# A hybrid mixing layer with a SwiGLU network: stores put off by a tile, a product order changed, and the passage into gate/up rearranged

## The chip, the cores and the metric

The kernel runs on one core of one Trainium2 chip. The metric is the device time of one execution in microseconds, the median over the runs. The engines are named as in the profile: PE (TensorE, matmuls), PEld (its weight loads), DVE (VectorE), ACT (ScalarE), POOL (GpSimd) and SP (SyncE, which here issues nearly all DMAs). Each engine takes its instructions in order, so an instruction that waits holds up everything behind it in its engine's queue. "The granted clock" is the share of full speed at which PE was allowed to run; its two levels here are 1.2 and 2.4 GHz (0.5 and 1.0).

## The reference, cut to what matters

There are 2048 tokens of width 1024, one sequence, one layer, float32.

```python
mod = silu(c) @ ada_w + ada_b            # six vectors: shift, scale, gate, twice
h = x * (1 + scale_m) + shift_m
z = h @ w_in                             # 512 columns each of cg, xin, bg, q, k, v, g
y_conv = bg * conv3(cg * xin)            # short causal convolution over tokens
q, k = rotary(q), rotary(k) * 128**-0.5  # 4 heads of 128
r = head_norm(retention(q, k, v))        # chunks of 128 tokens, decaying state
mix = concat(y_conv, silu(g) * r) @ w_out
x = layernorm(alpha * x + gate_m * mix) * ln1_g + ln1_b
h = x * (1 + scale_f) + shift_f
ff = (silu(h @ w_gate) * (h @ w_up)) @ w_down      # inner width 2816
out = layernorm(alpha * x + gate_f * ff) * ln2_g + ln2_b
```

## The kernel before, in words

**Arithmetic.** Each large product is made of three float16 matmuls that add up in float32: both operands are split into a rounded part (hi) and the rest (lo), and `mm3` (L135 to L137) issues hi·hi, hi·lo and lo·hi. A split is one ACT instruction (L130, hi) and one DVE instruction (L131, lo). The convolution's projection and gate/up multiply 2 x 2 blocks with seven products and not eight, so sums and differences of blocks (called planes for the activations) are made beforehand and the products are combined afterwards. A product is 12 matmuls of 512 columns, a gemm of the retention 24.

**Memory.** SBUF is cut into 24 pages of 128 x 2048 float32. `free` puts a page at the end of a list and `page` takes one from its front; `page(at=-1)` takes the last one, that which was freed most recently. Whoever writes a page waits for what still reads it, so the place in the list at which a page is freed decides whose transfer waits for whose.

**Order.** A planner puts the instructions of each engine in order by a simulated time, with the order of the program as the priority. `tc.issue_after(ins)` places what its block issues, on the engine of `ins`, behind that instruction.

**Stages.** After a start of some 125 us, the *retention* goes by tiles t of 128 tokens, t = 4 to 15, to some 460 us. A tile has four gemms (`gemm_ret(t, u)`: q, k, v, g), each evicted from PSUM into the tile's page: u = 0 by DVE (L705), u = 1 and 2 by ACT (L709), u = 3 by ACT with Silu (L711). Around them stand the rotary of t (L734 to L736 on DVE, then POOL), the transposes of t - 1 (L753, DMAs issued on SP), the scores of t - 1 (masked by DVE, L767), the state (L782), and y of t - 2 (matmuls L793, statistics L800 and L802, L804 to L807 on POOL, L810 on DVE), its transposed store through `ret_mix` (L832). Two tiles form a pair p; on every even tile the next pair's x, loaded at L231 on SP, is modulated (`ret_h`, L296, on ACT for p > 3) and split (`ret_hsplit`). The convolution needs seven planes of every pair. They are made in the tiles too: `h_more` stores the planes of the first split, makes sums on POOL (L344 to L347), splits them, and stores the other planes; `h_store` (L356) issues these DMAs on ACT. The pairs 4 to 7 leave this as a closure in `chores`; the pairs 0 to 3, whose x is loaded again, do it in the tiles 7, 10, 11 and 13 (`h_again`). The conditioning weights come through `ada_load` (on SP, `page(at=-1)`) and are summed by DVE (`ada_sum`, L199).

The *convolution* (some 460 to 710 us) has 12 pairs of a column block and a half of the tokens; each makes its seven products in the order 0, 5, 4, 1, 6, 3, 2 (`conv_pair`), with evictions on DVE (L973, L978, L982, L984) and ACT (L971, L975). Product 6 adds into the PSUM bank of product 5, product 1 into that of product 0, product 2 into that of product 4.

The *out-projection* (to some 875 us) goes over pairs of token tiles j = 0, 1, 4, 5, 6, 7, 2, 3. `op_half` adds one half (0: convolution, 1: retention) to y (L1307 on DVE), `norm1` normalises (statistics L1267 on DVE, scaling L1278 on ACT), `y_store` keeps y in DRAM (L1327), `h2_pair` scales it for the network (L1341 on DVE, L1342 on POOL) and makes the planes (L1347 to L1355), `h2_turn` transposes them (L1374, SP).

In the *passage* the weights of the first column blocks q of gate/up are scaled and split (`gu_split1`: L1412, L1413; `gu_split2`: differences L1421 to L1423, then L1426 on ACT and L1427 on DVE), and the first three blocks run: `gu(0, 1)`, `gu(1, 1)` and, once the last pair is there, `gu(0, 0)`. `gu` makes its seven products in the order A11, S2, S1, A12, A22, S3, S4; S3 adds into the bank of S2, which DVE first reads into u2 (L1465); S4 adds into that of S1 and A12 into that of A11, which ACT reads first (L1467, L1463). Gate/up runs to some 1590 us and the down-projection with the second norm to the end.

Of the kernel before, what the change touches and what calls it, by code (L numbers as in the profile page):

```python
# [11 lines left out]
F16 = mybir.dt.float16  # L12
# [28 lines left out]
def kernel(ctx: ExitStack, tc: tile.TileContext, xT, x, c, adaN, adaT, ada_b, w_ret, w_conv,  # L41
                             conv_w, w_out, ln1, ln1c, w_gu, w_dn, ln2, rope, consts, out):
    nc = tc.nc
# [340 lines left out]
    chores = []  # L384

    def h_more(p, pg, h):
        h_store(p, h, (0, 1, None, 3))
        h_sums(pg)
        g, _ = h_split(pg, hs[:, 0:1])
        h_store(p, g, (5, 2, 6, 4))  # L390
        free(pg, g)

    def h_again(p):

        pg = xt_pg.pop(p)
        for k in range(KT):
            modulate(pg.rearrange("p (k n) -> p k n", k=KT), k, True)
        h, _ = h_split(pg, hs[:, 0:1])
        h_more(p, pg, h)
        free(h)  # L400
# [288 lines left out]
    T1 = {}  # L689

    def gemm_ret(t, u):
# [258 lines left out]
    def conv_pair(u, b, done=lambda m: None):  # L950
# [125 lines left out]
    for t in range(4, NT):  # L1076
# [15 lines left out]
        gemm_ret(t, 1)  # L1092
        if t % 2 == 1 and p < 7:
            xt_load(p + 1)
# [23 lines left out]
        if end:  # L1118
            free(ropep, *ret_pages[4:6])
            hp_load(0, 4)  # L1120
            hp_load(0, 1)
            hp_load(0, 6)
        if t % 2 == 0 and p < 8:
            ret_h(p)
            ret_hsplit(p)
# [3 lines left out]
        if end:  # L1129
            free(*ret_pages[6:8])  # L1130
            hp_load(0, 3)
# [39 lines left out]
    ahead = [0, 5, 4, 1, 6, 3, 2]  # L1171
# [102 lines left out]
    def norm1(y):  # L1274
# [3 lines left out]
        nc.scalar.activation(y, y, AF.Identity, scale=rs, bias=nm)  # L1278
# [50 lines left out]
    def h2_pair(j, tp=None):  # L1329
# [4 lines left out]
        fp = yp[j] if tp else page()  # L1334
# [74 lines left out]
    def gu_split1(q):  # L1409
# [5 lines left out]
        gu_w[q] = {"A11": av[:, :, 0], "A12": av[:, :, 1], "S1": av[:, :, 2], "A22": av[:, :, 3], "pages": [wa]}  # L1415

    def gu_split2(q, eng):
        pg = gu_stage.pop(q)
# [10 lines left out]
        w = gu_w[q]  # L1429
# [8 lines left out]
    u32, ucount, gu_last, gu_pe = [], [0], [None], [None]  # L1438
# [3 lines left out]
    def gu(q, bl, between=None):  # L1442
# [28 lines left out]
        nc.scalar.activation(u[:, 0], pa, AF.Silu, scale=iv_g)  # L1471
        pd = new()
        prod(pd, "A22", T4, True, True)
        prod(pb, "S3", T3, False, True)
# [4 lines left out]
        prod(pc, "S4", B22, False, True)  # L1479
        nc.vector.tensor_add(u2, pc, u2)  # L1480
# [175 lines left out]
    order = (0, 1, 4, 5, 6, 7, 2, 3)  # L1656
    for i, j in enumerate(order):
# [10 lines left out]
        if i == 7:  # L1668
# [8 lines left out]
            gu_split2(0, nc.gpsimd)  # L1677
        for t in (2 * j, 2 * j + 1):
            if i < 7:
                op_half(t, 0)  # L1680
            op_half(t, 1)
            norm1(ytile(t))
# [8 lines left out]
        else:  # L1691
            y_store(j)
        if i == 5:
            gu_load(1)
    free(*wo_pages[2:])
    for i in range(2):
        gu_pages[i].append(page(F16, at=-1))
    gu_split1(1)
    gu_split2(1, nc.vector)
    free(*gu_pages[2])  # L1700
    gu_pages[2].clear()
    gu(0, 1)
# [11 lines left out]
    gu(1, 1)  # L1714
# [3 lines left out]
    gu_scale(2)  # L1718
# [4 lines left out]
    gu_scale(3)  # L1723
# [176 lines left out]
```

## Time and profile before

| | |
|---|---|
| median of 3 runs | 2106.2 us (2104.92 to 2108.79) |
| profiled execution | 2106.87 us |
| its span, first to last instruction | 2104.7 us |
| mean granted clock | 0.987 |
| matmuls | 9631 |
| data moved by DMA | 361.06 MB, 172 GB/s |

The span is what the trace covers; the execution's own time has some 2 us more around it. A busy time sums what an engine worked; an idle time before an instruction is shown in brackets with what ended it.

### The profile page before, as it was taken

To read this page: it belongs to the slowest core of one execution; us is meant where nothing else is said; L and a number is where in the kernel's file an instruction comes from. 1 tells how busy PE (TensorE), PEld (TensorE's weight loads), DVE (VectorE), ACT (ScalarE), POOL (GpSimd) and SP (SyncE) were. 2 spreads that over 40 slices of the span, in tenths; PEclk is the share of its full clock that TensorE was granted. 3 is DMA by queue.
4 is the path that set the end of the run, shared out by engine and by line. 5 is a ranking of instruction groups with operands and counts; after the bars stand their busy time and mean duration, and the time that the engine had idled before them with its cause. 6 is when DMAs were issued, how large, how long until landed. Compare 5 with 4: busy or idle time off the path is not lost.

```text
span 2104.7 us, 24640 instructions
## 1 busy us (share of the span) xinstructions
PE 2023.1 (96%) x9631; PEld 948.0 (45%) x9631; DVE 1463.8 (70%) x1793; ACT 666.9 (32%) x728; POOL 904.9 (43%) x751
## 2 busy tenths in 40 slices
PE   8899998989899999789999999999999999999998
PEld 3354554444344544334444444444444444444443
DVE  7898846567686577766678768877777354478564
ACT  5523443433422223332323223343433222212210
POOL 3554855555642377742323114544444143134232
PEclk9999999999999999999999999999999999999999
DMA  9048544576873298742444553434343665375321
GB/s 380 26 135 260 163 133 110 161 236 212 269 307 125 85 251 195 186 128 71 149 170 166 184 189 126 160 126 154 131 150 120 237 263 198 139 272 190 150 77 74
DMA packets 189492, 361.06 MB, mean 172 GB/s; under 512 B 118080, under 2 KB 118080, under 8 KB 166592
## 3 DMA queue, kind: packets, MB, share of 16 engines
q1 hardware_dynamic: 181168, 344.55, 49.1%
q10 hardware_dynamic: 8208, 14.95, 2.1%
q8 instruction: 75, 1.23, 0.2%
q14 instruction: 41, 0.34, 0.0%
HBM read 231.26 MB, written 100.93 MB: 158 GB/s over the span
## 4 chain that ended last, share of the span: by engine, by line
PE 42%; DVE 8%; POOL 5%; DMA 5%; issue 2%; ACT 2%; SPq 0%; POOLq 0%; DVEq 0%; ACTq 0%
PE mm L135 7%; PE mm L136 7%; PE mm L137 7%; PE ax L135 7%; PE ax L137 7%; PE ax L136 7%; DMA pg<-yscr 2%; DMA pg<-in_w_dn_dram 2%; POOL pg L1342 1%; DVE pg L1617 1%; ACT pg L1278 1%; DVE wdm L87 1%; DVE pg L1618 1%; DVE pg L1482 1%; POOL rs L1270 1%
## 5 line engine op out<-in xcount | busy, mean ns | idle before, releaser
L135 PE MATMUL mm<-pg,pg 128*128 128x512 f16 x1604 | 609.4, 382 | 18.4 <-ACT pg L1426 8.2
L136 PE MATMUL mm<-pg,pg 128*128 128x512 f16 x1604 | 611.2, 381 | 0.0
L137 PE MATMUL mm<-pg,pg 128*128 128x512 f16 x1604 | 609.5, 381 | 1.7 <-DVE pg L889 1.7
L135 PE MATMUL ax<-pg,pg 128*128 128x512 f16 x1220 | 462.9, 380 | 9.3 <-DVE t2k L973 3.8
L137 PE MATMUL ax<-pg,pg 128*128 128x512 f16 x1220 | 462.6, 380 | 1.5 <-DVE pg L889 1.5
L136 PE MATMUL ax<-pg,pg 128*128 128x512 f16 x1220 | 463.3, 380 | 0.0
L136 PEld LDWEIGHTS <-pg 128*128 128x128 f16 x2888 | 283.3, 98 | 350.4 <-issue 23.7
L135 PEld LDWEIGHTS <-pg 128*128 128x128 f16 x2888 | 283.3, 98 | 345.7 <-issue 9.5
L137 PEld LDWEIGHTS <-pg 128*128 128x128 f16 x2888 | 283.1, 98 | 340.7 <-issue 6.4
L1476 POOL TENSOR_TENSOR pg<-pg,t2k 128x512 f32<-128x512 f32 x44 | 57.9, 1315 | 383.2 <-DVE t2k L1475 207.6
L131 DVE SCALAR_TENSOR_TENSOR pg<-pg,p2s,pg 128x2048 f16<-128x2048 f32 (+1 forms) x42 | 95.9, 2294 | 134.5 <-ACT pg L130 134.4
L130 ACT ACTIVATE pg<-pg,p2s 128x2048 f16<-128x2048 f32 (+1 forms) x42 | 77.6, 1858 | 262.2 <-PE mm L136 114.1
L87 DVE TENSOR_REDUCE m<-pg 128x2 bf16<-128x2048 f32 (+1 forms) x38 | 86.3, 2275 | 20.9 <-DMA pg<-in_w_gu_dram 10.8
L525 PE MATMUL mm<-pg,pg 128*128 128x512 f16 x384 | 89.1, 387 | 5.6 <-DVE pg L533 2.5
L1481 ACT ACTIVATE pg<-t2k,ivg 128x512 f32<-128x512 f32 x44 | 31.6, 717 | 178.1 <-DVE t2k L1480 178.1
L1530 DVE TENSOR_TENSOR pg<-pg,pg 128x2048 f16<-128x2048 f32 (+1 forms) x22 | 46.3, 2103 | 44.6 <-ACT pg L1529 44.6
L1413 DVE TENSOR_TENSOR pg<-pg,pg 128x2048 f16<-128x2048 f32 x22 | 51.7, 2349 | 31.7 <-ACT pg L1412 31.7
L1529 ACT ACTIVATE pg<-pg 128x2048 f16<-128x2048 f32 (+1 forms) x22 | 37.3, 1697 | 99.6 <-DMA wscr<-pg 57.8
L131 DVE SCALAR_TENSOR_TENSOR pg<-pg,hs,pg 128x1024 f16<-128x1024 f32 x32 | 49.4, 1547 | 26.8 <-ACT pg L130 26.6
L1270 POOL TENSOR_SCALAR rs<-mv 128x1 f32<-128x1 f32 x32 | 30.5, 957 | 82.2 <-DVE mv L1268 79.6
L1583 POOL TENSOR_TENSOR pg<-pg,pg 128x2048 f32<-128x2048 f32 (+1 forms) x6 | 26.9, 4491 | 82.0 <-DVE pg L131 38.6
L525 PEld LDWEIGHTS <-pg 128*128 128x128 f16 x384 | 37.5, 99 | 52.4 <-issue 7.7
(278 smaller groups left out, 2782.7 us busy)
## 6 DMA issues: line engine op xcount, KB each, us to landing
pg<-wscr SPq DMA_DIRECT2D x28, 1024.0 KB, 4.8
pg<-in_w_gu_dram SPq DMA_DIRECT2D x22, 1024.0 KB, 4.9
uscr<-pg SPq DMA_DIRECT2D x44, 512.0 KB, 2.8
pg<-in_w_dn_dram SPq DMA_DIRECT2D x22, 1024.0 KB, 5.9
pg<-in_adaT_dram SPq DMA_DIRECT2D x21, 1024.0 KB, 8.2
wscr<-pg SPq DMA_DIRECT2D x77, 256.0 KB, 2.9
yscr<-pg SPq DMA_DIRECT2D x16, 1024.0 KB, 4.3
pg<-uscr SPq DMA_DIRECT2D x16, 1024.0 KB, 5.7
```

Source lines behind the costliest of these rows:

```text
L87: return nc.vector.tensor_reduce(dst, src, axis=AX.X, op=OP.max, apply_absolute_value=True).ins
L130: nc.scalar.activation(hi, src, AF.Copy, scale=s)
L131: nc.vector.scalar_tensor_tensor(lo, src, s, hi, op0=OP.mult, op1=OP.subtract)
L135: nc.tensor.matmul(ps, l_hi, r_hi, start=start, stop=False, skip_group_check=again)
L136: nc.tensor.matmul(ps, l_hi, r_lo, start=False, stop=False, skip_group_check=again)
L137: return nc.tensor.matmul(ps, l_lo, r_hi, start=False, stop=stop, skip_group_check=again).ins
L525: nc.tensor.matmul(ps, hv[:, a, k, o], w[:, k], start=n == 0 and k == k0, stop=n == 2 and k == k1 - 1)
L1270: nc.gpsimd.tensor_scalar(rs, mv[:, 1:2], EPS / (ALPHA * ALPHA), None, op0=OP.add)
L1413: nc.vector.tensor_sub(wa[:, 2048:], pg, wa[:, :2048])
L1476: nc.gpsimd.tensor_add(e5, e5, p1)
L1529: nc.scalar.activation(o[:, :n, 0], src, AF.Copy)
L1530: nc.vector.tensor_sub(o[:, :n, 1], src, o[:, :n, 0])
```

## The change

1. *Retention.* `h_more` no longer issues its stores: it makes the sums and the second split, and leaves both stores with the freeing of their pages as a closure in `stores`. The next tile runs these behind its eviction of u = 1. `ret_h` and `ret_hsplit` are placed behind the eviction of u = 2, and `h_again` or a chore behind that of u = 3. Chores are taken from the front, so pair 6 goes in tile 12 and pair 7 in tile 14; before, it was pair 7 and then pair 6.
2. *Convolution.* Product 3 comes before product 6, and the loads of the planes follow that order.
3. *Passage.* For the last pair both halves of both tiles run before the norm; the differences of `gu_split2(0)` are made by DVE and no longer by POOL; `gu_split2(1)` comes before the norm and before `gu_split1(1)`, which is placed behind the first ACT eviction of `gu(0, 1)`. The norm's scaling of the last pair is placed behind the Silu of that block. `gu(0, 1)` and `gu(1, 1)` run their products in the order A11, S1, A12, A22, S2, S4, S3. The last pair's `h2_pair` writes into another page and no longer into y itself, with two of its temporaries in y's page. The scaling of the blocks 2 and 3 is placed behind the last matmul so far.

```diff
-    def h_more(p, pg, h):
-        h_store(p, h, (0, 1, None, 3))
+    def h_more(p, pg, h, *done):
         h_sums(pg)
         g, _ = h_split(pg, hs[:, 0:1])
-        h_store(p, g, (5, 2, 6, 4))
-        free(pg, g)
+        free(pg)
+
+        def store():
+            h_store(p, h, (0, 1, None, 3))
+            h_store(p, g, (5, 2, 6, 4))
+            free(g, *done)
+        stores.append(store)
...
-        h_more(p, pg, h)
-        free(h)
+        h_more(p, pg, h, h)
...
-            nc.scalar.activation(dst, ps, AF.Copy, scale=iv)
+            evicted[0] = nc.scalar.activation(dst, ps, AF.Copy, scale=iv).ins
         else:
-            nc.scalar.activation(dst, ps, AF.Silu, scale=iv)
+            evicted[0] = nc.scalar.activation(dst, ps, AF.Silu, scale=iv).ins
...
         prod(pa, 1, False, True)
+        pd = new()
+        prod(pd, 3, True, True)
         prod(pb, 6, False, True)
         nc.vector.scalar_tensor_tensor(p1, pb, iv, p1, op0=OP.mult, op1=OP.add)
         nc.gpsimd.tensor_add(e5, e5, p1)
-        pd = new()
-        prod(pd, 3, True, True)
         nc.vector.scalar_tensor_tensor(p1, pd, iv, p1, op0=OP.mult, op1=OP.add)
...
         gemm_ret(t, 1)
+        with tc.issue_after(evicted[0]):
+            while stores:
+                stores.pop()()
...
         if t % 2 == 0 and p < 8:
-            ret_h(p)
-            ret_hsplit(p)
+            with tc.issue_after(evicted[0]):
+                ret_h(p)
+                ret_hsplit(p)
...
-        if t in AGAIN:
-            h_again(AGAIN.index(t))
-        elif chores:
-            chores.pop()()
+        with tc.issue_after(evicted[0]):
+            if t in AGAIN:
+                h_again(AGAIN.index(t))
+            elif chores:
+                chores.pop(0)()
...
-    ahead = [0, 5, 4, 1, 6, 3, 2]
+    ahead = [0, 5, 4, 1, 3, 6, 2]
...
-        nc.scalar.activation(y, y, AF.Identity, scale=rs, bias=nm)
+
+        def scaled():
+            nc.scalar.activation(y, y, AF.Identity, scale=rs, bias=nm)
+        return scaled
...
-        fp = yp[j] if tp else page()
+        fp = tp or page()
...
-            t = [tp[:, i * 512:(i + 1) * 512] for i in range(3)]
+            t = [owner[id(hl[1])][1][:, 1536:2048], yp[j][:, :512], yp[j][:, 512:1024]]
...
-    def gu(q, bl, between=None):
+    def gu(q, bl, between=None, late=False):
...
-        nc.scalar.activation(p1, pa, AF.Copy)
-        prod(pb, "S2", T2, True, True)
-        nc.vector.tensor_add(u2, pb, p1)
+        gu_act[0] = nc.scalar.activation(p1, pa, AF.Copy).ins
+        if not late:
+            prod(pb, "S2", T2, True, True)
+            nc.vector.tensor_add(u2, pb, p1)
...
         prod(pd, "A22", T4, True, True)
+        if late:
+            prod(pb, "S2", T2, True, True)
+            nc.vector.tensor_add(u2, pb, p1)
+            prod(pc, "S4", B22, False, True)
+            nc.vector.tensor_add(u2, pc, u2)
         prod(pb, "S3", T3, False, True)
...
-            gu_split2(0, nc.gpsimd)
+            gu_split2(0, nc.vector)
+            for t in (2 * j, 2 * j + 1):
+                op_half(t, 1)
+            free(*wo_pages[2:])
+            for n in range(2):
+                gu_pages[n].append(page(F16, at=-1))
+            gu_split2(1, nc.vector)
...
-            norm1(ytile(t))
+                op_half(t, 1)
+            scaled = norm1(ytile(t))
+            if i < 7:
+                scaled()
+            else:
+                last_rows.append(scaled)
...
-    gu_split1(1)
-    gu_split2(1, nc.vector)
+    gu(0, 1, late=True)
+    with tc.issue_after(gu_act[0]):
+        gu_split1(1)
+    with tc.issue_after(gu_act[1]):
+        for scaled in last_rows:
+            scaled()
+    y_store(3)
...
-    gu(0, 1)
...
-    gu(1, 1)
+    gu(1, 1, late=True)
...
-    gu_scale(2)
+    with tc.issue_after(gu_pe[0]):
+        gu_scale(2)
...
-    gu_scale(3)
+    with tc.issue_after(gu_pe[0]):
+        gu_scale(3)
```

## Rows read from the trace of the kernel before

**Rows 1.** The page's first part: busy time, share of the span and instructions by engine.

```profile
PE 2023.1 (96%) x9631; PEld 948.0 (45%) x9631; DVE 1463.8 (70%) x1793; ACT 666.9 (32%) x728; POOL 904.9 (43%) x751
```

**Rows 2.** Busy by stretch: length; PE, PEld, DVE, ACT, POOL; PEclk, DMA, GB/s.

```profile
175.00:250.00 75.00, 68.00 (x351) 36.46 (x350) 63.43 (x106) 31.82 (x51) 47.34 (x43) 0.92 0.63 203
...
325.00:400.00 75.00, 66.04 (x339) 35.06 (x338) 45.15 (x73) 30.42 (x43) 39.27 (x32) 0.93 0.47 127
400.00:450.00 50.00, 45.50 (x231) 23.75 (x229) 29.89 (x65) 11.17 (x16) 19.03 (x18) 0.97 0.60 173
540.00:582.00 42.00, 34.83 (x154) 15.11 (x153) 27.02 (x29) 14.37 (x17) 23.89 (x18) 0.97 0.77 274
...
845.00:883.00 38.00, 27.21 (x126) 11.88 (x125) 29.90 (x39) 12.85 (x13) 32.27 (x28) 0.96 0.57 159
883.00:945.00 62.00, 56.24 (x246) 24.25 (x245) 43.87 (x52) 21.66 (x25) 23.95 (x22) 0.94 0.60 154
```

**Rows 3.** PE's waits, 125 to 475 us: total, times, longest.

```profile
PE ax L793 <- DVE pg L767: 15.3, 6, 4.3
PE ax L793 <- DVE g L125: 2.8, 1, 2.8
```

**Rows 4.** ACT's waits in the same stretch.

```profile
ACT pg L296 <- DMA pg<-in_xT_dram: 40.3, 6, 11.1
```

**Rows 5.** Timeline of ACT, 326 to 354 us: start, duration, instruction, idle before.

```profile
329.30 0.85 ACTq L356 DMA_DIRECT2D hcscr<-pg  x2
340.75 4.04 ACT L296 ACTIVATE pg<-pg,mod,msc 128x256 f32<-128x256 f32 x8 [11.12 <-DMA pg<-in_xT_dram]
...
345.73 0.67 ACT L709 ACTIVATE pg<-mm,iv 128x512 f32<-128x512 f32 x1
```

**Rows 6.** Timeline of SP's queue, same stretch.

```profile
335.79 0.33 SPq L231 DMA_DIRECT2D pg<-in_xT_dram  x1
```

**Rows 7.** Timeline of DVE, same stretch.

```profile
347.07 1.22 DVE L734 TENSOR_TENSOR pg<-pg,pg 128x1024 f32<-128x1024 f32 x1
...
352.21 0.74 DVE L767 SCALAR_TENSOR_TENSOR pg<-ax,pg,mask 128x512 f32<-128x512 f32 x1
```

**Rows 8.** Busy by stretch of line L199 alone: length, DVE, PEclk, DMA, GB/s.

```profile
125.00:220.00 95.00, 24.32 (x32) 0.95 0.70 219
220.00:450.00 230.00, 0.00 (x0) 0.96 0.50 143
```

**Rows 9.** Timeline of PE, 574 to 580 us.

```profile
578.69 0.38 PE L135 MATMUL ax<-pg,pg 128*128 128x512 f16 x1 [3.80 <-DVE t2k L973]
```

**Rows 10.** Timeline of DVE, 573 to 580 us.

```profile
574.40 1.23 DVE L199 SCALAR_TENSOR_TENSOR pg<-pg,pg 128x1024 f32<-128x1024 f32 x1 [4.13 <-DMA pg<-in_adaT_dram]
...
577.89 0.74 DVE L973 SCALAR_TENSOR_TENSOR t2k<-ax,ivc,t2k 128x512 f32<-128x512 f32 x1
```

**Rows 11.** Timeline of PE, 872 to 914 us.

```profile
882.80 0.61 PE L135 MATMUL mm<-pg,pg 128*128 128x512 f16 x1 [8.22 <-ACT pg L1426]
...
887.59 0.59 PE L137 MATMUL mm<-pg,pg 128*128 128x512 f16 x2
...
905.29 0.38 PE L137 MATMUL ax<-pg,pg 128*128 128x512 f16 x1
```

**Rows 12.** Timeline of POOL, 872 to 884 us.

```profile
872.57 1.26 POOL L1421 TENSOR_TENSOR pg<-pg 128x512 f32<-128x512 f32 x1
...
877.92 3.31 POOL L1423 TENSOR_TENSOR pg<-pg,pg 128x512 f32<-128x512 f32 x1
```

**Rows 13.** Timeline of DVE, 884 to 916 us.

```profile
886.30 0.69 DVE L1421 TENSOR_TENSOR pg<-pg 128x512 f32<-128x512 f32 x1
...
892.24 0.67 DVE L1465 TENSOR_TENSOR t2k<-mm,t2k 128x512 f32<-128x512 f32 x1
...
903.04 4.64 DVE L1341 TENSOR_TENSOR pg<-pg,pg 128x512 f32<-128x512 f32 x4 [4.42 <-DMA yscr<-pg]
...
913.43 0.68 DVE L1465 TENSOR_TENSOR t2k<-ax,t2k 128x512 f32<-128x512 f32 x1
```

More of the change, by code (lines that the diff above doesn't have):

```diff
@@ L382, in ret_hsplit @@
             chores.append(lambda: h_more(p, pg, h))
-    chores = []
-    def h_more(p, pg, h):
-        h_store(p, h, (0, 1, None, 3))
+    chores, stores = [], []
+    def h_more(p, pg, h, *done):
         h_sums(pg)
         g, _ = h_split(pg, hs[:, 0:1])
-        h_store(p, g, (5, 2, 6, 4))
-        free(pg, g)
+        free(pg)
[4 more added lines that the diff above has]
+        stores.append(store)
     def h_again(p):
@@ L689 @@
     T1 = {}
+    evicted = [None]
     def gemm_ret(t, u):
@@ L1121 @@
             hp_load(0, 1)
-            hp_load(0, 6)
+            hp_load(0, 3)
         if t % 2 == 0 and p < 8:
-            ret_h(p)
-            ret_hsplit(p)
+            with tc.issue_after(evicted[0]):
+                ret_h(p)
+                ret_hsplit(p)
         if t == NT - 2:
@@ L1130 @@
             free(*ret_pages[6:8])
-            hp_load(0, 3)
+            hp_load(0, 6)
             hp_load(0, 2)
@@ L1414, in gu_split1 @@
         av = wa.rearrange("p (a s k n) -> p a s k n", a=2, s=4, k=4)
-        gu_w[q] = {"A11": av[:, :, 0], "A12": av[:, :, 1], "S1": av[:, :, 2], "A22": av[:, :, 3], "pages": [wa]}
+        w = gu_w.setdefault(q, {"pages": []})
+        w.update({"A11": av[:, :, 0], "A12": av[:, :, 1], "S1": av[:, :, 2], "A22": av[:, :, 3]})
+        w["pages"].insert(0, wa)
     def gu_split2(q, eng):
-        pg = gu_stage.pop(q)
+        pg = gu_stage[q]
         a = pg.rearrange("p (s n) -> p s n", s=4)
@@ L1428, in gu_split2 @@
         bv = ws[:, :3072].rearrange("p (a s k n) -> p a s k n", a=2, s=3, k=4)
-        w = gu_w[q]
+        w = gu_w.setdefault(q, {"pages": []})
         w.update({"S2": bv[:, :, 0], "S3": bv[:, :, 1], "S4": bv[:, :, 2], "tmp": owner[id(ws)][1][:, 1536:2048]})
@@ L1436, in gu_done @@
         gu_pages[1].append(ws)
-    u32, ucount, gu_last, gu_pe = [], [0], [None], [None]
+    u32, ucount, gu_last, gu_pe, gu_act = [], [0], [None], [None], [None, None]
     uscr = [[dram.tile([2, P, NCH, 512], F32, name=f"uscr{b}{r}") for r in range(2)] for b in range(2)]
     um = const.tile([P, 2, NFF], F32, name="um")
-    def gu(q, bl, between=None):
+    def gu(q, bl, between=None, late=False):
         w = gu_w[q]
@@ L1470, in gu @@
         prod(pa, "A12", B21, False, True)
-        nc.scalar.activation(u[:, 0], pa, AF.Silu, scale=iv_g)
+        gu_act[1] = nc.scalar.activation(u[:, 0], pa, AF.Silu, scale=iv_g).ins
         pd = new()
         prod(pd, "A22", T4, True, True)
+        if late:
[3 more added lines that the diff above has]
+            nc.vector.tensor_add(u2, pc, u2)
         prod(pb, "S3", T3, False, True)
@@ L1478, in gu @@
         nc.vector.scalar_tensor_tensor(u[:, 0], p1, iv_u, u[:, 0], op0=OP.mult, op1=OP.mult)
-        prod(pc, "S4", B22, False, True)
-        nc.vector.tensor_add(u2, pc, u2)
+        if not late:
+            prod(pc, "S4", B22, False, True)
+            nc.vector.tensor_add(u2, pc, u2)
         nc.scalar.activation(u[:, 1], u2, AF.Silu, scale=iv_g)
@@ L1656 @@
     order = (0, 1, 4, 5, 6, 7, 2, 3)
+    last_rows = []
     for i, j in enumerate(order):
@@ L1680 @@
                 op_half(t, 0)
-            op_half(t, 1)
-            norm1(ytile(t))
+                op_half(t, 1)
[4 more added lines that the diff above has]
+                last_rows.append(scaled)
         if j % 2 == 1:
@@ L1690 @@
                 h2_turn(j)
-        else:
-            y_store(j)
         if i == 5:
             gu_load(1)
-    free(*wo_pages[2:])
-    for i in range(2):
-        gu_pages[i].append(page(F16, at=-1))
-    gu_split1(1)
-    gu_split2(1, nc.vector)
+    gu(0, 1, late=True)
[5 more added lines that the diff above has]
+    y_store(3)
     free(*gu_pages[2])
     gu_pages[2].clear()
-    gu(0, 1)
     for pl in (B11, T2, T1_, B21, T3, T4, B22):
```

## The prediction

> **What bounds the kernel now.** I read the busy times first: TensorE is busy 2023.1 of 2104.7 us and no other engine comes near [rows 1]. So nothing is won but what TensorE loses: idle time, and matmuls that run at the lower of its two clocks. 2023.1 us over 9631 matmuls are 0.21 us each, thus 2.5 us for a product of 12 and 5.0 us for a gemm of 24. Then I read the busy times by stretch, for the three places that the change touches [rows 2]. The loss of a stretch is its length less PE's busy time, plus (1 - PEclk) times its length for the lower clock, which comes in windows right behind the long stalls. For the retention this makes 7.0 + 6.0 = 13.0 us (175 to 250), 9.0 + 5.3 = 14.2 (325 to 400) and 4.5 + 1.5 = 6.0 (400 to 450); for the convolution 7.2 + 1.3 = 8.4 (540 to 582); for the passage 10.8 + 1.5 = 12.3 (845 to 883) and 5.8 + 3.7 = 9.5 (883 to 945). That is 63 us in all, and DVE, at 63.4 of 75 us in the first and 73.8 of 100 in the passage, is the engine that could take over.
>
> The waits say what PE stood for: in the tiles, six times for DVE's masking of the scores, L767, 15.3 us, once 4.3 [rows 3]. Followed back, that longest one shows a chain. ACT issues the last of a pair's stores at 329.30; the load of the next x page goes out on SP at 335.79 [rows 6], its page being one that those stores read; ACT stands 11.12 us for it at L296 and works 4.04 us on it; the evictions L709 of the running tile stand behind that in ACT's queue, the first at 345.73 [rows 5]; DVE's rotary needs them, starts at 347.07, and L767 comes behind it at 352.21 [rows 7]. L296 stood 40.3 us for x loads, in six waits [rows 4].
>
> **The change part by part.** No matmul is added or taken away; all is order, pages and one engine.
>
> *Retention.* The modulation is now queued behind the eviction of u = 2, so it can't stand in front of that tile's two L709, and the chain above is cut at its middle: ACT may wait for x, the rotary does not. The stores are the same seven per pair; two cost ACT 0.85 us [rows 5], so seven cost 3.0 us, now behind the eviction of u = 1. ACT has the 5.0 us of gemm u = 2 for them and is busy 30.4 of 75 us [rows 2], so I cost them at nothing; if that cover is gone, the eviction of u = 2 is up to 3.0 us late and the scores of the tile before with it. The pairs now go in their order: 12 stores, then 14. Written out by hand over tiles 4 to 15, the list of free pages gives three of the x loads (pair 7, and pairs 2 and 3 again) a page that no store reads; before, they got a store's. Of the 14.2 us in 325 to 400 I credit two thirds, 9.5: bounds 0 (the stall only moves) and 14.2. Of the 13.0 in 175 to 250 I credit 2: there DVE is 63.4 of 75 us full, and 24.32 us of L199, the conditioning sums, stand there up to 220 and none after [rows 8]; bounds 0 and 13.0. Of the 6.0 in 400 to 450 nothing: the same pages wait for the same convolution loads. New waits: two pages that now follow a tile's transposes or put-off stores, 0 to 7 us (7 is half of 14.2, one stall with its clock); I take 2.5. Together 9.
>
> *Convolution.* Product 6 adds into the bank of product 5 and must wait until DVE has read it (L973). With product 3 ahead of it there are three products between and not two, so 2.5 us more cover. The long stall, 3.80 us [rows 9], is DVE's: L199 with its 1.2 us twice and more stand before L973 at 577.89 [rows 10]. 2.5 of 3.8 goes, and with it half of the lower clock behind it (1.3, counted 0.8): 3.3. What is late next is the same L973, 1.3 us. Bounds 0 (another sum before L973) and 5.1.
>
> *Passage.* The 8.22 us before gate/up wait for the rounding L1426 of the second weight split [rows 11], whose subtractions on POOL take 1.26, 1.26 and 3.31 = 5.8 us (rows of the first and the last) [rows 12]; DVE does one in 0.69 [rows 13], 2.1 for three. With it product S2 stands fifth, three products (7.6 us) later. Both say that this stall goes; with the lower clock after it, 10 of the 12.3. The Trainium skill (SBUF — State Buffer, section "SBUF: two separate sides") says that DVE with two SBUF inputs and GpSimd hold a port pair as a lock for a whole instruction; the 3.31 us beside the like 1.26 agree with it, and by that rule the moved subtractions may hold POOL up to 2.1 us, which would make the whole sum some 2 us smaller.
>
> The price stands in the same place. S3 adds into the bank that S2 filled, so it waits for DVE's L1465. Before, S1, A12 and A22 lay between; now S4 alone, 2.5 us. L1465 ran at 892.24 where S2 ended by 888.0, and at 913.43 where it ended by 905.5 [rows 11, 13]: ready 4.9 and 8.6 us after S2, 2.4 and 6.1 us too late for a cover of 2.5. But nothing needed it earlier, and it is itself 0.67 us. So 0 to 2.4 and 0 to 6.1; I take 1.5 each, 3 together, nearer to what its own length gives, since DVE is fuller than before. What waits behind PE then is all of gate/up.
>
> In the second half, DVE stood 4.42 us for the store of y before the last pair's scaling L1341 [rows 13]; that pair now writes into another page, so the wait goes and its seven transposes, on which the third block waits, come earlier by up to as much. The norm's scaling on ACT is put behind the Silu of A12 and so leaves ACT free for evictions in front of it. Of the 9.5 us there 1.75 is clock behind the first stall, already counted; half of the remaining 7.7 I credit, 3.8 (bounds 0 and 7.7). Passage: 10 + 3.8 - 3 = 10.8.
>
> *The sum:* 9 + 3.3 + 10.8 = 23 us. The profiled execution took 2106.87 us (its span of 2104.7 and 2.2 around it), so 2083.9 by it; the median of the runs is 0.7 lower, hence **2083 us**.
>
> **The rivals.** (a) *The retention's stalls only move.* DVE has rotary, transposes' split, scores and y in one queue; taking ACT out of it may leave PE waiting for L767 as before. For it: L767 is the last of DVE's items in each tile. Against: DVE is 45 of 75 us busy where the longest stall is. 14 us remain: 2092.
>
> (b) *The passage exchanges one wait for another.* S3 stands 2.4 + 6.1 us and each time the low clock follows, 1.7 as behind the stall of 883: 12 in all against 13.8 won: 2 remain, with the other parts 2092; with (a) as well, 2101. For it: DVE gets 2.1 us more; if the loss all went it would be 75.9 busy of some 82 us. Against: S4 does not need L1465, and DVE has loads to wait for.
>
> (c) *More goes than counted:* with pages free later the conditioning sums leave 175 to 220, so half of those 13.0 and the 400 to 450 stall go too: 2065. For it: L199 is all in front of 220. Against: nothing in the diff moves their calls.
>
> (d) *Slower.* The loads of the conditioning weights take the page at the list's end (`page(at=-1)`); by the same list that is, in four tiles (7, 8, 9, 11), a page whose store was put off and which it still reads. SP then stands until it lands, and behind it in SP's queue stand the transposes and the next x load; or DVE stands at L199, with rotary and L767 behind. A stall of 7 us in each: 28, and the 9 are not had. 28 - 14 = 14 slower, **2120**; it decides from the third tile (3 x 7 - 14 = 7). For it: 329.30 to 335.79 shows how long a load stands behind stores. Against: the load has a tile of some 20 us (four gemms of 5.0) before its sum is due. That the change doesn't do what it says (the planner gives other engines the old order) is within (a).
>
> **How the numbers follow.** Forecast, 2073 to 2089: 0.42. (a) alone 0.12, (b) alone 0.14, both 0.08 (half of it under 2102), (c) 0.10, (d) 0.14. What a measurement can tell is 0.2%, 4.2 us: under 2102.0 faster, above 2110.4 slower. Faster: 0.42 + 0.12 + 0.14 + 0.04 + 0.10 = 0.82; slower: most of (d), 0.13; within: 0.05. The range leaves out (d) and a rest of (c): 2062 to 2106, which also holds the low bounds of the unknown costs; the forecast's own range is 2073 to 2089.
>
> **What would show it.** Right: no wait of L709 behind L296 in the tiles; L767's waits under 7 us; the stall by 578 about 1.3 us; no stall over 2 us between the last out-projection matmul and the first of gate/up; PE's waits for L1465 under 2 us each. Wrong: PE idle in 325 to 400 as before but at other times (a); waits on L1465 of 3 us and more (b); L199 spread over tiles 7 to 11 with PE stalls beside it, or SP waiting for stores in front of transposes (d).

## The result, and the profile after

The changed kernel takes 2093.1 us (median of 4 runs, 2092.12 to 2093.36) where the kernel before takes 2106.5 in the same comparison: a ratio of 0.9935 (95% interval 0.9917 to 0.9952), 13.4 us less. Forecast were 23 us less; the direction and the range held, the size did not, and the places from which the time comes are in part others than those named. The profiled execution took 2092.12 us, its span 2090.3.

Line numbers move: L709 is L713 in the changed kernel, L715 the Silu, L753 is L757, L767 is L771, L888 is L892, L971 is L975, L973 is L977, L1157 is L1166, L1307 is L1319, L1426 is L1440, L1427 is L1441, L1465 is L1492, L1467 is L1483.

The page's first part, for the changed kernel (answers to [rows 1]; PE does the same matmuls in 6 us less, at a mean granted clock of 0.990 and not 0.987):

```profile
PE 2017.0 (96%) x9631; PEld 945.5 (45%) x9631; DVE 1467.6 (70%) x1796; ACT 666.6 (32%) x728; POOL 897.0 (43%) x748
```

The busy times by stretch, each stretch cut at about the same work as in [rows 2] (columns as there; the first and the third hold 12 and 14 matmuls of 512 columns more than before, some 3 us of work each):

```profile
175.00:243.00 68.00, 65.88 (x368) 35.66 (x366) 46.73 (x94) 25.84 (x41) 33.62 (x43) 1.00 0.58 160
312.50:391.00 78.50, 65.72 (x336) 34.33 (x334) 56.24 (x86) 36.01 (x53) 50.81 (x37) 0.93 0.50 141
391.00:442.00 51.00, 49.08 (x258) 25.92 (x257) 37.60 (x61) 17.48 (x25) 23.15 (x20) 0.97 0.65 205
533.00:574.00 41.00, 34.59 (x151) 14.78 (x150) 24.40 (x27) 14.81 (x17) 24.26 (x18) 0.96 0.71 258
838.00:929.00 91.00, 80.07 (x371) 35.70 (x370) 70.84 (x81) 29.07 (x32) 50.23 (x42) 1.00 0.65 172
```

By the prediction's own measure (idle time of PE and the lower clock) the first stretch lost 13.0 us before and loses 2.1 now; the second 14.2 and now 12.8 + 5.5 = 18.3; the third 6.0 and now 3.4; the convolution's 8.4 and now 8.0; the two of the passage 21.8 together, now 10.9. So by this measure the tiles gave their time where 2 us were credited, and took some back where 9.5 were.

A sharper measure: every trace holds the same 8472 matmuls of 512 float16 columns, and at the places named here the same number of them lies ahead, so the start of the n-th compares the kernels place by place. In us against the kernel before (the last two columns are described below):

| start of | before at | changed | tiles alone | sums spread | stores at once | block not queued |
|---|---|---|---|---|---|---|
| tile 6 | 183.0 | -0.5 | -0.1 | 0.1 | -0.3 | -0.7 |
| tile 7 | 215.8 | -6.7 | -4.7 | -8.4 | -1.3 | -5.3 |
| tile 8 | 240.3 | -7.1 | -5.1 | -8.8 | -1.7 | -5.6 |
| tile 9 | 268.7 | -11.4 | -9.4 | -7.3 | -6.0 | -10.0 |
| tile 11 | 318.1 | -12.6 | -10.6 | -4.3 | -4.7 | -10.3 |
| tile 12 | 343.4 | -9.8 | -7.5 | -3.6 | -7.5 | -0.5 |
| tile 13 | 375.8 | -15.2 | -14.4 | -0.4 | -7.8 | -8.8 |
| tile 14 | 404.6 | -8.9 | -4.3 | -5.1 | -7.1 | -13.5 |
| convolution | 461.6 | -8.2 | -4.3 | -6.4 | -3.9 | -12.6 |
| gate/up | 871.8 | -7.1 | -1.1 | -5.8 | -4.3 | -11.5 |
| its fifth block | 963.0 | -16.5 | -1.4 | -6.0 | -13.3 | -20.9 |
| last matmul | 2096.1 | -14.8 | 0.8 | -2.9 | -9.9 | -16.4 |

How far such a column can be trusted: the kernel with the convolution's change alone has the instructions of the kernel before up to the convolution, and its profile stands 2.4 us off it at tile 7 and 0.1 at tile 11. The kernel with the passage's change alone loses 2.4 us in a convolution that was not touched. And six kernels have the whole tiles' part (the changed one, two of the parts below and three of the later runs): they begin the convolution 4.3 to 8.2 us early, with the changed kernel at the upper end. So a step of 2 us is no finding unless it comes back in several kernels, and a sum over all tiles is known to some 4 us.

PE's waits in the tiles, 125 to 460 us of the changed kernel (answers to [rows 3]): L771 (L767 before), which made 15.3 us, is gone from the list, and three other waits stand at its head. The third, for the rounding of the first convolution weights, stands at the start of the convolution (3.41 us in front of its first product, 1.13 in it); its cause is open.

```profile
PE ax L136 <- DMA pg<-pg: 5.7, 2, 5.5
PE mm L135 <- ACT pg L713: 5.4, 1, 5.4
PE mm L135 <- ACT pg L892: 4.5, 2, 3.4
```

The conditioning sums (answers to [rows 8]), and the wait of SP in front of their loads:

```profile
125.00:220.00 95.00, 9.40 (x12) 1.00 0.57 169
220.00:450.00 230.00, 16.08 (x20) 0.97 0.59 177
```

```profile
SPq L191 <- DMA hcscr<-pg: 30.7, 3, 16.7
```

This is the mechanism of rival (d): the loads take pages whose put-off stores still read them, and SP stands 30.7 us for it. But nobody needed those sums early. What the wait did was to take 14.9 of 24.3 us of DVE's work out of the stretch in which DVE was 63.4 of 75 us full, and that is what rival (c) said.

The wait of 5.4 us is a new one. Timelines of ACT, POOL and PE in tile 11 (start, duration, instruction, idle before):

```profile
327.89 1.15 ACT L130 ACTIVATE pg<-pg,hs 128x1024 f16<-128x1024 f32 x1 [7.19 <-POOL pg L345]
...
332.88 0.67 ACT L713 ACTIVATE pg<-mm,iv 128x512 f32<-128x512 f32 x1
```

```profile
324.37 1.27 POOL L344 TENSOR_TENSOR pg<-pg 128x512 f32<-128x512 f32 x1
...
326.59 1.27 POOL L345 TENSOR_TENSOR pg<-pg 128x512 f32<-128x512 f32 x1
```

```profile
333.60 0.59 PE L135 MATMUL mm<-pg,pg 128*128 128x512 f16 x1 [5.41 <-ACT pg L713]
```

The second split of the planes is queued on ACT behind the eviction of u = 3, and so ahead of the next tile's evictions. It waits 7.19 us for POOL's sums, and the eviction L713, at 332.88, waits behind it. The change took a wait for a load out of ACT's queue (L296's 40.3 us are gone) and put a wait for POOL into it (ACT stands 35.9 us for L345 in the tiles, and stood 5.6).

The wait of 5.5 us is for transposes (those of tile 12, in tile 13). Two DMA views of the changed kernel, for 358 to 367 and 381 to 391 us (issues, KB each, median us to landing), and PE's row:

```profile
pg<-pg SPq DMA_TRANSPOSE x2, 3.2
```

```profile
hcscr<-pg ACTq DMA_DIRECT2D x3, 256.0 KB, 3.9
pg<-pg SPq DMA_TRANSPOSE x1, 5.5
```

```profile
387.61 0.26 PE L136 MATMUL ax<-pg 128*128 128x128 f16 x1 [5.49 <-DMA pg<-pg]
```

In the second view the transpose follows seven put-off stores (issued from 378.81 on, 3.77 us) and lands 5.5 us after its issue instead of 3.2. That is 2.3 of the 5.49 us. The other 3.2 are its late issue: the transpose of the hi halves went out at 376.61, that of the lo halves only at 382.07, when PE already came for it. Its split stood on DVE behind three splits of planes:

```profile
373.24 5.46 DVE L131 SCALAR_TENSOR_TENSOR pg<-pg,hs,pg 128x1024 f16<-128x1024 f32 x3
378.62 3.43 DVE L131 SCALAR_TENSOR_TENSOR pg<-pg,pg,pg 128x512 f16<-128x512 f32 x2
```

That it was the stores which made the landing late is not shown: two transposes of the same kernel, issued at 285.31 and 287.27 with at most one store under way, took 6.1 and 7.5 us.

The convolution's fifth pair, PE and DVE:

```profile
545.13 0.38 PE L135 MATMUL mm<-pg,pg 128*128 128x512 f16 x1 [2.00 <-ACT t2k L975]
...
558.51 0.39 PE L135 MATMUL ax<-pg,pg 128*128 128x512 f16 x1 [2.64 <-ACT pg L892]
560.64 0.39 PE L135 MATMUL ax<-pg,pg 128*128 128x512 f16 x1 [1.53 <-ACT pg L892]
```

```profile
544.04 2.67 DVE L1166 TENSOR_TENSOR pg<-pg,pg 128x2048 f32<-128x2048 f32 x1 [7.09 <-DMA pg<-in_w_out_dram]
...
551.65 0.14 DVE L117 TENSOR_SCALAR s<-e 128x1 int32<-128x1 int32 x1
```

The 3.80 us of [rows 9] for L973 are gone. In front of their place PE now waits for L892, the rounding of the sixth block's weights. Their scale (L117) stands on DVE behind L1166, which waits 7.09 us for the output weights. POOL makes the differences of these weights only after that, and had ended its products of the conditioning weights (L468) at 543.3:

```profile
538.67 4.66 POOL L468 TENSOR_TENSOR pg<-pg,pg 128x1024 f32<-128x1024 f32 x2 [2.49 <-DMA pg<-in_adaT_dram]
...
553.91 1.26 POOL L885 TENSOR_TENSOR pg<-pg 128x512 f32<-128x512 f32 x1 [0.78 <-ACT pg L884]
```

The passage, PE (answers to [rows 11]):

```profile
878.11 0.38 PE L135 MATMUL mm<-pg,pg 128*128 128x512 f16 x1 [1.96 <-DVE pg L1319]
...
883.75 0.38 PE L135 MATMUL mm<-pg,pg 128*128 128x512 f16 x1 [2.90 <-ACT pg L1483]
...
891.42 0.38 PE L135 MATMUL mm<-pg,pg 128*128 128x512 f16 x1 [1.89 <-DVE t2k L1492]
```

No wait reaches the 8.22 us of before and the clock stays at 1.00 through the whole stretch. S3 waits 1.89 for the copy of S2 in the first block and not at all in the second. The planner had put 14 matmuls of the second block (886.34 to 889.52) in front of that S3. The 2.90 are of S4, which adds into the bank of S1 and waits until ACT has read that (L1483). The reading stands in ACT's queue behind the second block's rounding, which waits for DVE's differences:

```profile
881.73 1.48 ACT L1440 ACTIVATE pg<-pg 128x1536 f16<-128x1536 f32 x1 [7.02 <-DVE pg L1437]
```

### The profile page after: what moved, and what is told of

Same layout as the page of the kernel before. It is cut to its first block, busy times and chain, and to the rows that moved or that the text cites. A ratio compares the mean times of both kernels' runs of the same rounds, so it can differ in the third digit from the quotient of the medians.

```text
span 2090.3 us, 24590 instructions
## 1 busy us (share of the span) xinstructions
PE 2017.0 (96%) x9631; PEld 945.5 (45%) x9631; DVE 1467.6 (70%) x1796; ACT 666.6 (32%) x728; POOL 897.0 (43%) x748
## 3 DMA queue, kind: packets, MB, share of 16 engines
q8 instruction: 75, 1.23, 0.2%
## 4 chain that ended last, share of the span: by engine, by line
PE 41%; DVE 9%; DMA 5%; POOL 4%; issue 2%; ACT 2%; SPq 0%; POOLq 0%; DVEq 0%; ACTq 0%
PE mm L135 7%; PE mm L137 7%; PE mm L136 7%; PE ax L135 7%; PE ax L137 7%; PE ax L136 7%; DMA pg<-yscr 2%; DMA pg<-in_w_dn_dram 2%; DVE pg L1639 1%; DVE pg L1504 1%; DVE wdm L87 1%; DVE pg L1441 1%; DVE pg L1640 1%; ACT pg L1289 1%; DVE pg L1499 1%
## 5 line engine op out<-in xcount | busy, mean ns | idle before, releaser
L137 PEld LDWEIGHTS <-pg 128*128 128x128 f16 x2888 | 283.4, 98 | 341.4 <-issue 10.8
L87 DVE TENSOR_REDUCE m<-pg 128x2 bf16<-128x2048 f32 (+1 forms) x38 | 86.4, 2276 | 16.1 <-DMA pg<-in_w_gu_dram 12.5
L131 DVE SCALAR_TENSOR_TENSOR pg<-pg,hs,pg 128x1024 f16<-128x1024 f32 x32 | 50.2, 1593 | 18.4 <-ACT pg L130 18.3
```

The lines of the kernel that those rows point to most:

```text
L87: return nc.vector.tensor_reduce(dst, src, axis=AX.X, op=OP.max, apply_absolute_value=True).ins
L131: nc.vector.scalar_tensor_tensor(lo, src, s, hi, op0=OP.mult, op1=OP.subtract)
L137: return nc.tensor.matmul(ps, l_lo, r_hi, start=False, stop=stop, skip_group_check=again).ins
```

## The experiments

Each ratio is against the kernel before on the same chip, with its 95% interval. Over the chips the kernel before took 2106.5 to 2110.2 us, so kernels from different chips are compared by their ratios (the changed kernel: 0.9935). There are two questions: do the three parts add up, and what in each part makes its time.

**The parts alone.** Edits: the first part of the diff shown ahead, with the old order of the plane loads (3 after 6); its second part, whose core is

```diff
         prod(pa, 1, False, True)
+        pd = new()
+        prod(pd, 3, True, True)
         prod(pb, 6, False, True)
```

its third part; and the first with the third.

> The kernel before with the retention's part alone. Theory (the three parts add up): the convolution begins 8.2 us earlier, as in the changed kernel, and nothing else is won: 8 us less. If the late start of L199 (the conditioning sums) and not the order of ACT is what won, L199's busy time before 220 us falls from 24.3 to some 9.4 us here too. Rival (the retention's gain is lost again later): under 4 us less, with a new wait in the convolution.

Measured: 2105.8, ratio 0.9990 (0.9980 to 0.9999). The tiles win 10.6 us by tile 11, and 4.3 are left when the convolution begins. L199 has 9.42 us before 220, as expected. The rest goes in the convolution, where PE still waits 3.96 for L977, and in gate/up. So the rival holds for the end, and the theory up to tile 11 alone: the convolution begins 4.3 and not 8.2 us early, and this part alone is worth 2 us.

> The kernel before with product 3 ahead of product 6 alone. Prediction as made: the 3.80 us stall by 578 us shrinks to 1.3 and its lower clock goes, 3.3 us less. Rival: the new order makes the planner put the maximum over the output weights ahead of the scale of the last convolution weights on DVE, as in the changed kernel, and PE waits for the rounding L888 there instead: within 1 us of before.

Measured: 2107.9, ratio 0.9996 (0.9987 to 1.0005): the rival. The fifth pair loses 3.0 us, the sixth wins 3.0, and the waits are the changed kernel's: 2.65 and 1.54 for L888, and none for L973.

> The kernel before with the passage's part alone. Theory (parts add up): 9.3 us less from the first to the third block of gate/up, less 1.5 given back in gate/up: 7.8 us less in all. Rival (the passage lives on the 8 us that the retention's earlier end leaves to its loads): under 5 us less, with PE waiting for a load or a transpose.

Measured: 2098.7, ratio 0.9960 (0.9945 to 0.9975). From the first to the fifth block of gate/up it wins 9.4 us; the changed kernel wins 9.3 there. The theory holds: the passage does not live on what comes ahead of it.

> The changed kernel with the old order of the convolution's products (6 before 3). If the new order costs as much as it saves (planner's order of the weights' scale): within 1 us of the changed kernel, 2093. If the new order saved its 3.3 us and something of the retention's part took them: 3 us slower than the changed kernel, 2096. If the new order is what brings the new wait and nothing more: 3 us faster, 2090.

Measured: 2095.4, ratio 0.9948 (0.9931 to 0.9964), between the first two expectations: some 2 us slower than the changed kernel, by an interval that also holds none. In its trace the convolution loses 2.8 us against the kernel before, in the changed one 0.4. That the new order saves 2 us beside the tiles' part is not shown by this: the kernel with the passage alone, where neither the tiles nor the convolution were touched, loses 2.4 there too.

Do the parts add up? Alone they save 2.1 us, nothing and 9.1 us, together 11 where the whole saves 13; the intervals do not tell the two apart.

**What won in the tiles.**

```diff
 # kernel before; ev0: the DVE eviction of u = 0
-            ada_sum(t + 3)
+            with tc.issue_after(ev0[0]):
+                ada_sum(t + 3)
```

> The kernel before, with each tile's conditioning sum (L199) queued on DVE behind that tile's eviction of u = 0 and nothing else changed, so that the 24.3 us of sums that stood before 220 us spread over the tiles 5 to 12. Theory (the changed kernel won its first 11 us of the tiles because the put-off stores delayed the conditioning loads and so took the sums out of tiles 4 to 6): most of the 10.6 to 12.6 us by the start of tile 10 here too, 8 or more. Rival (they were won by taking the x loads' wait out of ACT's queue ahead of the evictions): under 3 us by tile 10.

Measured: 2102.3, ratio 0.9975 (0.9966 to 0.9985). Busy time of L199 by stretch in this kernel:

```profile
125.00:220.00 95.00, 4.73 (x8) 1.00 0.65 180
220.00:450.00 230.00, 17.97 (x24) 0.96 0.55 169
```

Tile 6 alone wins 8.5 us (changed kernel: 6.2). The 4.3 us that the changed kernel wins in tile 8 are not won; that tile loses 1.5. So the theory holds for the first step and not for the second, and by tile 10 it is 4.3 us, between both expectations.

```diff
-        stores.append(store)
+        store()
```

> The changed kernel with the planes stored as soon as they are split, not put off to the next tile; the queueing behind evictions stays. Theory: the pages come free as before, so all the sums stand before 220 us again and the win by tile 10 falls from 12.6 to under 5 us; the 5.5 us stall in tile 12, where the transposes' second half lands 4.0 us after its issue beside seven put-off stores, goes: 5 us back. In all some 2 to 5 us slower than the changed kernel. Rival (the queueing behind evictions makes the win): the win by tile 10 stays at 10 or more and the kernel is faster than the changed one.

Measured: 2096.5, ratio 0.9943 (0.9925 to 0.9961). L199 in this kernel:

```profile
125.00:220.00 95.00, 22.55 (x32) 0.98 0.68 209
220.00:450.00 230.00, 0.00 (x0) 0.97 0.55 152
```

In all, by the ratios, some 2 us slower than the changed kernel, with intervals that overlap. With the stores at once the sums stand early again and tile 6 wins 1.0 us and not 6.2; tile 8 wins its 4.3 all the same. So the 11 us by tile 9 have two makers: the put-off stores, by way of the sums (tile 6), and the queueing (tile 8). That the stall for transposes would go did not come true: PE waits for transposes 9.4 us in two waits (5.8 and 3.6, in tiles 12 and 13), so such stalls come without the delay too.

```diff
-        with tc.issue_after(evicted[0]):
-            if t in AGAIN: ...
-            elif chores: ...
+        if t in AGAIN: ...
+        elif chores: ...
```

> The changed kernel with the block after gemm u = 3 (the second split of a pair's planes, or a whole pair again) not queued behind the eviction of u = 3. Theory: the 5.41 us stall in tile 11, where the eviction stands on ACT behind a split that waits for POOL's sums (L345, 7.2 us), goes, with its lower clock: 5 to 8 us earlier by the start of tile 12, and some of it kept to the end. Rival (the planner puts that split ahead of the evictions too, as it did with L296 before): the same stall, within 1 us.

Measured: 2088.6, ratio 0.9906 (0.9892 to 0.9921); its interval and the changed kernel's just overlap. The wait for L713 is gone, but tile 11 is 9.8 us longer, not shorter, by another wait. PE and DVE there:

```profile
319.05 0.79 PE L797 MATMUL ax<-pg,pg 128*128 128x128 f32 x2 [5.89 <-DVE g L125]
```

```profile
312.59 5.68 DVE L131 SCALAR_TENSOR_TENSOR pg<-pg,hs,pg 128x1024 f16<-128x1024 f32 x3
318.19 0.14 DVE L123 TENSOR_SCALAR g<-g 128x1 f32<-128x1 f32 x1
318.26 0.74 DVE L771 SCALAR_TENSOR_TENSOR pg<-ax,pg,mask 128x512 f32<-128x512 f32 x1
```

Three splits in a row hold L771, PE's old releaser (the profile names L125, which stands right behind it on DVE; what the matmul reads is L771's). Tiles 12 and 13 give it back (8.3 and 4.7 us), and the convolution begins 12.6 us early and not 8.2. Neither theory had this: where the block stands decides which tile pays. Over the tiles 11 to 15, the three kernels without the queueing of the block take 2.0 to 2.3 us less than the kernel before, the two whose tiles were not touched 2.1 less as well, and the six with the whole tiles' part 2.7 to 6.2 more: the queued block costs there, and without it the rest of the part wins nothing in these tiles. Tile 8 keeps its 4.3 us, here and with the stores at once. So by elimination it is the queueing of `ret_h` and `ret_hsplit` behind u = 2 which wins them; a kernel with that alone was not run.

**What took the convolution's gain.**

```diff
-                wo_max(0)
+                with tc.issue_after(conv_last[6]):   # last DVE eviction of the 7th pair
+                    wo_max(0)
```

> The changed kernel with the maximum over the output weights (L1166 and its reduction, on DVE) queued behind the last DVE eviction of the seventh convolution pair; in the changed kernel DVE stood 7.8 us for that load in the fifth pair, with the scale of the last convolution weights behind it. Theory: PE's waits for the weights' rounding in the fifth pair (2.64 and 1.53) and for L975 (2.00) go, with the lower clock: 4 us less up to the seventh pair, 2089. Rival (POOL's part of the conditioning sums, L468, holds that chain): within 1 us of the changed kernel.

Measured: 2093.9, ratio 0.9933 (0.9918 to 0.9947): nothing in all, as the rival said, but not for its reason. From the start of the fifth to that of the seventh pair this kernel wins 4.7 us (the changed one 0.7) and waits no more for the rounding, as in the theory; pairs 8 and 9 lose 4.6. So in the changed kernel L1166 held the weights' scale (L117 at 551.65, here at 548.42), though a part of what is won is that PE comes to the fifth pair 3.1 us later here.

```diff
 # on top of "block not queued"
-                wo_max(0)
+                with tc.issue_after(cw_scaled[0]):   # the scale of the 6th block's weights
+                    wo_max(0)
```

> The changed kernel with the block after gemm u = 3 not queued behind its eviction, and with the maximum over the output weights queued on DVE behind the scale of the last convolution weights (so that the scale no longer stands behind that load). Theory: the tiles as without the queueing (2088.6), and PE's waits for L892 in the fifth convolution pair (2.8 and 1.1, with the lower clock) go without the 4.6 us that came back in the eighth and ninth pair when the maximum was queued three pairs later: 3 us less, 2085 to 2086. Rival (the maximum's 9 us on DVE cost the same wherever they stand): 2088 to 2090.

Measured: 2091.9, ratio 0.9918 (0.9903 to 0.9933), not better than without this edit (0.9906). It tests neither theory nor rival, as in the kernel that it starts from the scale (L117) already stood ahead of the maximum (here L1165), which did not wait:

```profile
539.90 0.15 DVE L117 TENSOR_SCALAR s<-e 128x1 int32<-128x1 int32 x1
...
546.62 2.28 DVE L1165 TENSOR_TENSOR pg<-pg,pg 128x2048 f32<-128x2048 f32 x1
```

Yet PE waits for the same rounding there, 2.80 and 1.10 us (with this edit 2.77 and 1.18). In that kernel, "block not queued", another engine is in front of it, POOL:

```profile
539.95 5.67 POOL L468 TENSOR_TENSOR pg<-pg,pg 128x1024 f32<-128x1024 f32 x2
545.55 1.20 POOL L1005 COPY carry<-pg 128x2 f32<-128x2 f32 x1
546.83 2.14 POOL L118 TENSOR_SCALAR ivc<-e 128x1 f32<-128x1 f32 x1
...
549.09 1.27 POOL L885 TENSOR_TENSOR pg<-pg 128x512 f32<-128x512 f32 x1
...
553.02 1.26 POOL L888 TENSOR_TENSOR pg<-pg,pg 128x512 f32<-128x512 f32 x1
```

POOL makes products of the conditioning weights (L468) before the four differences from which the weights are rounded.

```diff
 # on top of "block not queued"; cw_pooled: the last of the four differences
-                ada_sum_both(15 + n)
+                with tc.issue_after(cw_pooled[0]):
+                    ada_sum_both(15 + n)
```

> As again_free (the changed kernel with the block after gemm u = 3 not queued), with POOL's conditioning products L468 queued behind the differences of the last convolution weights. Theory (POOL's in-order queue is the chain that ate the new product order's gain: in again_free the weights were scaled on ACT by 543.1, but their four differences stood behind L468 and ran from 549.1 to 554.3): PE's waits for L892 in the fifth pair (2.80 and 1.10, with their clock) go, the stretch from the fifth to the seventh pair is 3 to 5 us shorter than in again_free: 2084 to 2086. Rival (DVE's or ACT's part is late anyway): within 1 us of again_free's 2088.6; or the same 9 us of L468 hold the next pairs' POOL work and the time comes back by the tenth pair.

Measured: 2089.1, ratio 0.9901 (0.9885 to 0.9918). POOL in this kernel, and POOL, DVE and PE in the ninth pair:

```profile
541.99 1.27 POOL L887 TENSOR_TENSOR pg<-pg 128x512 f32<-128x512 f32 x1 [2.03 <-ACT pg L886]
...
545.91 1.27 POOL L890 TENSOR_TENSOR pg<-pg,pg 128x512 f32<-128x512 f32 x1
```

```profile
605.79 6.61 POOL L468 TENSOR_TENSOR pg<-pg,pg 128x1024 f32<-128x1024 f32 x2
```

```profile
606.84 3.36 DVE L199 SCALAR_TENSOR_TENSOR pg<-pg,pg 128x1024 f32<-128x1024 f32 x1
...
610.14 3.35 DVE L199 SCALAR_TENSOR_TENSOR pg<-pg,pg 128x1024 f32<-128x1024 f32 x1
...
613.42 0.74 DVE L986 SCALAR_TENSOR_TENSOR t2k<-ax,ivc,t2k 128x512 f32<-128x512 f32 x1
```

```profile
614.21 0.27 PE L99 MATMUL ax<-ident,m 128*128 128x128 f16 x2 [2.89 <-DVE t2k L986]
```

The theory's stretch and the rival's second half both came true. The differences end at 547.2 and not 554.3, no wait for the rounding is left, and fifth and sixth pair are 7.4 us shorter than before (2.2 with L468 ahead of the differences). By the start of the tenth pair 4.7 are lost again, where the same products and sums now stand in front of an eviction. So POOL's queue was the chain in the kernels whose block is not queued, as DVE's L1166 was in the changed kernel, and moving either moves the loss.

**What made the passage.**

```diff
-    gu(0, 1, late=True)
+    gu(0, 1)
...
-    gu(1, 1, late=True)
+    gu(1, 1)
```

> The changed kernel with the first two blocks of gate/up in the old order of products (S2 second). Theory: the later place of S2 carries at least half of the passage's 9.3 us, because the second split on DVE ends (875.5) long after A11 begins (864.7): 5 us slower than the changed kernel, 2098, with PE waiting for L1440 or L1441; S3's wait of 1.9 goes. Rival (the move of the split to DVE did it all, the order only adds S3's wait): 1 to 2 us faster.

Measured: 2095.6, ratio 0.9932 (0.9918 to 0.9947), by the ratio the same as the changed kernel: neither 5 us slower, as in the theory, nor faster. The passage still wins 8.1 of its 9.3 us. PE waits where expected, 7.1 us, and the first block wins next to nothing (0.3 us, where the changed kernel wins 4.3); in the two blocks behind it PE gets the time back (7.7 us, where the changed kernel wins 5.0), as S4 and S3 then wait for nothing:

```profile
872.54 0.61 PE L135 MATMUL mm<-pg,pg 128*128 128x512 f16 x1 [3.98 <-ACT pg L1440]
876.66 0.61 PE L137 MATMUL mm<-pg,pg 128*128 128x512 f16 x1 [3.09 <-DVE pg L1441]
```

```diff
-            gu_split2(0, nc.vector)
+            gu_split2(0, nc.gpsimd)
```

> The changed kernel with the second split of block 0 on POOL again. Theory: with S2 fifth, 5.8 us of POOL behind the last pair's planes (POOL is busy with them to 871.1 in the changed kernel) make it ready at some 879 and not 871, where S2 begins at 878: 0 to 3 us slower than the changed kernel. Rival (the split on POOL is the whole 8.22 us stall of before, whatever the order): 6 us slower or more.

Measured: 2093.1, ratio 0.9930 (0.9914 to 0.9947): the passage wins 9.1 of 9.3 us, and the theory holds. So either edit can be taken back at a cost of 0.2 to 1.2 us. Whether the two stand in for each other, or the passage's remaining edits make the gain without either, is open: a kernel with neither was not run.

## Why the prediction came out as it did

*The tiles, 9 us forecast, 8.2 came (4.3 to 8.2 in the six kernels with this part), by other steps.* That the numbers are near is luck. In the changed kernel the tiles 6 to 10 win 12.1 us, where 2 were credited (175 to 250); the tiles 11 to 15 lose 4.4, where 9.5 less 2.5 were. Right: L296's wait for x is gone from ACT, L767 has left PE's list, and tile 12, where the gain was forecast, is 5.4 us shorter. Wrong is, first, the step that credited 175 to 250 us with 2 of 13. Tile 6 wins 6.2 there because the put-off stores hold back the conditioning loads, and tile 8 wins 4.3, by elimination through the queueing of `ret_h`. The text had the first mechanism twice. Rival (c) had it with the right sign and a chance of 0.10, and set against it that nothing in the diff moves the calls of the sums; the wait for pages moved them. (Its time of 2065 does not follow from its terms: half of 13.0 and 6.0 make 12.5 us, so 2071 at the least.) Rival (d) had it with the sign reversed: SP's wait was counted as a stall for PE, and it was not asked whether the sums were urgent. DVE's 63.4 of 75 us in that stretch, also in the text, was the reason that they should better wait. Wrong is, second, the price of the new waits. The block queued behind u = 3 has no term in the sum; it brings POOL's sums into ACT's queue ahead of L713 (5.41 with its clock). The lo halves' transpose goes out late and lands late (5.49). The 2.5 us for new waits were the term too small: tiles 11 and 13 lost 2.8 and 6.3. And the seven stores, put at 3.0 us of ACT, take 3.77 in tile 13 and 6.12 in tile 12.

*The convolution, 3.3 us forecast, none came.* The cover worked: the wait for L973 is gone, more than the 2.5 of 3.8 us that were counted, and the sixth pair is 3.0 to 3.7 us shorter in each kernel with the new order and the old place of its side work. What failed is "What is late next is the same L973, 1.3 us". Late next were the weights of the sixth block: scale on DVE, differences on POOL, rounding on ACT. In the changed kernel they stand behind 7 us of a wait for the output weights, in the kernels with the block not queued behind 5.7 us of POOL's products. The profile of before showed that chain only as a wait of 1.24 us for the rounding's other half, and it was not followed through the engines.

*The passage, 10.8 us forecast, 9.3 came.* The first stall went; taking back either of the two means named for it costs at most 1.2 us, so which edit the gain needs is open. The second half's 3.8 came: the third block wins 3.8 in the changed kernel, and 3.5 to 4.4 in every kernel with the passage's part. S3's price was put at 3.0 and measured 1.9, within its bounds, but with the help of the 14 matmuls that the planner put in front of it; a cover of S4 alone was assumed. Not foreseen are three waits in the first block, 5.6 us: 2.90 of S4 for ACT's reading (L1483), which stands behind the second split, L1440; 1.96 for an eviction of the out-projection, L1319; and 0.75 for ACT's reading of A11. Rival (b) was right that waits take the place of the stall, and wrong about the clock: no wait here was followed by a stretch at half clock.

*Between*, a wait of 2.40 us for a DVE addition in gate/up (at 1142.6) with its clock gave back 3.7 us; it stands in five of the profiles (2.0 to 2.4 us) and is 0.6 to 1.7 us in the others. Its cause is open. Of the 8 us by which the sum was too large (23 against the 14.8 between the two profiles), 3.8 are the convolution's, 1.5 the passage's, 0.8 the tiles', and the rest lies in gate/up and the out-projection.

*The version that stands best.* The three kernels with the block after u = 3 not queued have ratios of 0.9906, 0.9901 and 0.9918 (2088.6, 2089.1 and 2091.9 us): 4 to 7 us less than the changed kernel's 0.9935, though the intervals overlap. With what the tiles 11 to 15 show, the queueing does not pay for `h_again` and the chores.

## What to carry to other kernels

A wait on a queue costs only what is due behind it, so before pricing a new wait ask when its data is needed: here waits of 30.7 us in all won some 5 us in the tile behind them, by moving work that nobody was waiting for out of the crowded stretch. Queueing a block behind an eviction also puts its waits in front of the next eviction; queue what has its inputs, and leave free what waits for a third engine. And where a stall is covered, follow the next-late operand back through all its engines, since here two moves of the side work, on two engines, won 4 to 5 us in the fifth and sixth pair and lost nearly all of it by the tenth.

## What the runs showed of the hardware

A DVE sum of two SBUF inputs that takes 1.22 us alone (1.23 in [rows 10]) took 3.36 and 3.35 while POOL worked on L468, and POOL's two products took 6.61 us there where two take 4.66 at 538.67 in the changed kernel. That agrees with the Trainium skill (SBUF — State Buffer, section "SBUF: two separate sides"), by which one of the two stands until the other's instruction is through. The changed kernel's transposes of the tiles landed 3.2 us after their issue with no store under way (at 360.90 and 362.17), and 5.5 behind seven stores issued just before (at 382.07).
